# The pace of the second group's output projection beside the first group's FFN, 0.5 to 3.0

## The chip, the cores and the metric

The kernel runs on one core of a Trainium2 chip. The metric is the device time of one execution in microseconds (us); the table below gives the median of three runs and the time of the one execution that was profiled. Engines are named as the profile names them: PE is TensorE (matmuls and transposes), DVE is VectorE, ACT is ScalarE, POOL is GpSimd, SP is the engine that issues most DMAs.

## What is computed

One decoder layer over 1024 prompt tokens and 64 sample tokens, width 1024. Only its end matters here: the mixer's output times `w_out` is added to `x`, then a norm and a SwiGLU FFN (2816 wide) follow, then a last norm.

```python
x = x + mix                                   # mix = mixed @ w_out
hf = rmsnorm(x, norm_ffn)
x = x + (jax.nn.silu(hf @ w_gate) * (hf @ w_up)) @ w_down
...
y_prompt = rmsnorm(xp, norm_final)
y_sample = rmsnorm(xs, norm_final)
```

## The kernel before

The tokens are worked in two groups: group 0 is prompt tokens 0 to 511 (four blocks of 128), group 1 is prompt tokens 512 to 1023 (four blocks, here t4 to t7) and the 64 sample tokens (here s). Every float32 product is made of three matmuls of a high and a low part (`hi*hi`, `hi*lo`, `lo*hi`), so each weight block that is loaded into `wraw` is split: ACT writes `whi` (L223), DVE writes `wlo` (L224). `wraw` has two buffers, `whi` and `wlo` have three each (`WB`, `WH`, `WL`, L64 to L66).

`outproj_b` (L1220) is the second half of the output projection. For each token block it loads `mt` and the earlier sum `x`, transposes `mt` on PE (L1178), and splits the result into `nat_hi` (ACT, L1228) and `nat_lo` (DVE, L1229). Then for each of four column parts c0 to c3 it loads and splits 4 x 256 weights and makes one group of 12 matmuls for each token block (8 for s), which DVE adds to `x` (L1238). Each group needs one of two PSUM banks `pm`.

`ffn_norm` (L1251) then norms each block by `norm_T` (L285): ACT squares and sums (L288), DVE makes the inverse root in nine instructions on one value per row (L213 to L219) and scales the block (`xn`, L289), PE transposes it in eight (L294), ACT writes `act_hi` (L223) and DVE `act_lo` (L224). For s there is a `join` first (L1241).

`ffn` (L1261) makes gate and up products of 24 matmuls each (`pm<-act_hi,whi`, 288 columns wide in group 1: t4, t5 and a quarter of t6 in the first half, the rest and s in the second), then the down product (`pm<-whi,hh`), added to `x` by L1320. In the last block of group 0 the two `w_down` parts stay split in two of the three `whi` buffers until the end, because the token blocks go outermost (t3 to t0, two groups of six matmuls each); after each block `final` norms it: a square on ACT (L1272), the nine DVE instructions, a scaling (L1277) and the store to `y_prompt` from ACT's queue. `far_rows` copies 1.5 MB pieces of `cache_win_v` to the output from SP's queue.

All of this is emitted by Python generators that yield units of estimated work. `beside(main, (side, pace))` (L1385) takes one step of the main generator and lets each side run until it has used pace times the units of that step. The Tile framework then schedules what is emitted, and on each engine the order is fixed in the program. The end of the kernel:

```python
op = pool(st1, "h1", "right")
x2 = op.tile([128, 5, D], F32, name="x2", bufs=1)
out1 = Side(outproj_b(1, op, x2), ffn_norm(1, op, x2), ahead=O7)
beside(dense, (out1, R10))
st0.close()
...
beside(out1, (far, 0.3))
beside(Side(ffn(1, op, x2, hp)), (far, 0.3))
```

`dense` is group 0's chain, of which the last FFN block is left here. What of `out1` is not used up beside `dense` is emitted by the line with `far`. `out1` has 5 x 1.5 + 20 x 1.3 + 5 x 3.0 = 48.5 units.

Of the kernel before, what the change touches and what calls it, by code (L numbers as in the profile page):

```python
# [37 lines left out]
R7 = 1.4  # L38
R8 = 1.1
R9 = 1.07  # L40
R10 = 0.5
R11 = 2.27
R12 = 2.0

# [102 lines left out]
def body(tc, I, O, C, off):  # L147
# [1072 lines left out]
    def outproj_b(F, tp, x2):  # L1220

        hi, lo = act_nat(tp, F)
        for tok in toks(F):
            i, rows, col = tok
            sp.dma_start(x2[:, col // 128], xa[F][col:col + 128])

            def fill(h_, l_, v):
                act.activation(h_, v, AF.Copy, scale=nB)  # L1228
                dve.scalar_tensor_tensor(l_, v, nB, h_.bitcast(F32), op0=OP.mult, op1=OP.subtract)  # L1229
            mixed_T(tp, hi, lo, tok, mix[2 + F][(i % 4) * 128:(i % 4 + 1) * 128] if i < 8 else mixs[1], fill)  # L1230
            yield 1.5
        for c in range(4):
            w = wsplit(w_out[:, 4:8, c * 256:(c + 1) * 256], 4, 256)
            for i, rows, col in toks(F):
                ps = mbank()[:, :256]
                nat_mm(his(hi), his(lo), w, 4, rows, col, ps, True, True)
                xv = x2[:, col // 128, c * 256:(c + 1) * 256]
                dve.tensor_tensor(xv, ps, xv, op=OP.add)  # L1238
                yield 1.3
# [11 lines left out]
    def ffn_norm(F, tp, x2):  # L1251
        wbc = bcast_row(tp, I["norm_ffn"], "wffn")
        hi, lo = act_pair(tp, 576 if F else 512)
        for i, rows, col in toks(F):
            if rows == 64:
                join(tp, x2, True)
            norm_T(tp, x2[:rows, col // 128], rows, wbc, hi, lo, col)
            yield 3.0
        normed[F] = hi, lo
# [125 lines left out]
    def beside(main, *sides, until=None):  # L1385

        left = until
        while main.live and (until is None or left > 0):
            x = next(main.g, None)
            if x is None:  # L1390
                main.live = False
                break
            if until is not None:
                left -= x
            for side, pace in sides:
                side.run(x * pace)
# [89 lines left out]
# [3 lines that stand above are left out]
# [35 lines left out]
```

## Time and profile before

| | us |
|---|---|
| median of three runs (1784.21 to 1785.14) | 1784.65 |
| the profiled execution, its own time | 1786.49 |
| its span in the trace | 1784.7 |
| PE busy in the span | 1697.0 (95%) |
| DVE busy | 1150.2 (64%) |
| ACT busy | 679.4 (38%) |
| mean DMA rate | 182 GB/s |

PE is the busy engine almost everywhere. The time of interest is where group 0's FFN ends and group 1's begins, some 1294 to 1362 us into the span. The granted clock there is given by the profile as a share of the full clock: 1.00 is 2.4 GHz and 0.50 is 1.2 GHz.

### The profile page before, as it was taken

To read this page: it belongs to the slowest core of one execution; us is meant where nothing else is said; L and a number is where in the kernel's file an instruction comes from. 1 tells how busy PE (TensorE), PEld (TensorE's weight loads), DVE (VectorE), ACT (ScalarE), POOL (GpSimd) and SP (SyncE) were. 2 spreads that over 40 slices of the span, in tenths; PEclk is the share of its full clock that TensorE was granted. 3 is DMA by queue.
4 is the path that set the end of the run, shared out by engine and by line. 5 is a ranking of instruction groups with operands and counts; after the bars stand their busy time and mean duration, and the time that the engine had idled before them with its cause. 6 is when DMAs were issued, how large, how long until landed. Compare 5 with 4: busy or idle time off the path is not lost. (4 is left out here: it accounts for less than half of the span.)

```text
span 1784.7 us, 27958 instructions
## 1 busy us (share of the span) xinstructions
PE 1697.0 (95%) x10462; PEld 1464.7 (82%) x10462; DVE 1150.2 (64%) x2829; ACT 679.4 (38%) x1379; POOL 78.2 (4%) x200
## 2 busy tenths in 40 slices
PE   4999999997999999999999989999998999999997
PEld 4988789996766668878887778888887999999996
DVE  6978966866776757797666546676576444343435
ACT  4545434441423353676421134454234223131222
POOL 1000000001001000000011001111100000000000
PEclk9999999998999999999998999999998999999999
DMA  8645556468898867534299678798494333241321
GB/s 272 182 145 159 162 179 171 116 200 271 266 282 256 256 208 225 188 104 118 66 284 287 180 224 256 248 304 274 133 325 154 128 95 95 59 130 36 107 72 65
DMA packets 309569, 324.96 MB, mean 182 GB/s; under 512 B 28221, under 2 KB 260669, under 8 KB 307754
## 3 DMA queue, kind: packets, MB, share of 16 engines
q1 hardware_dynamic: 297754, 275.64, 51.6%
q0 software_dynamic: 10304, 43.08, 6.8%
q10 hardware_dynamic: 1376, 4.46, 0.7%
q8 instruction: 82, 1.34, 0.3%
q14 instruction: 53, 0.43, 0.1%
HBM read 251.31 MB, written 105.63 MB: 200 GB/s over the span
## 5 line engine op out<-in xcount | busy, mean ns | idle before, releaser
L198 PE MATMUL pm<-act_hi,whi 128*128 128x288 f32 (+1 forms) x1056 | 349.4, 331 | 0.2 <-ACT act_hi L223 0.2
L198 PE MATMUL pm<-act_lo,whi 128*128 128x288 f32 (+1 forms) x1056 | 348.1, 330 | 0.0
L198 PE MATMUL pm<-act_hi,wlo 128*128 128x288 f32 (+1 forms) x1056 | 347.4, 329 | 0.0
L223 ACT ACTIVATE whi<-wraw 128x1024 fp32r<-128x1024 f32 x182 | 192.8, 1059 | 381.8 <-PE pm L198 275.8
L224 DVE TENSOR_TENSOR wlo<-wraw,whi 128x1024 fp32r<-128x1024 f32 x182 | 222.3, 1222 | 123.8 <-ACT whi L223 123.3
L198 PE MATMUL pm<-xh,whi 128*128 128x320 f32 (+2 forms) x672 | 230.6, 343 | 11.5 <-ACT whi L223 8.6
L198 PE MATMUL pm<-xl,whi 128*128 128x320 f32 (+2 forms) x672 | 228.4, 340 | 0.1
L198 PE MATMUL pm<-xh,wlo 128*128 128x320 f32 (+2 forms) x672 | 226.7, 338 | 0.2
L198 PEld LDWEIGHTS pm<-act_hi,whi 128*128 128x128 f32 x1056 | 199.2, 189 | 18.4 <-issue 2.1
L198 PEld LDWEIGHTS pm<-act_hi,wlo 128*128 128x128 f32 x1056 | 199.3, 189 | 14.5 <-issue 0.5
L198 PEld LDWEIGHTS pm<-act_lo,whi 128*128 128x128 f32 x1056 | 199.3, 189 | 14.2 <-issue 0.2
L198 PEld LDWEIGHTS pm<-xh,whi 128*128 128x128 f32 x672 | 129.1, 192 | 25.9 <-ACT whi L223 9.1
L1320 DVE TENSOR_TENSOR x<-pm,x 128x256 f32<-128x256 f32 (+1 forms) x148 | 79.9, 543 | 98.2 <-PE pm L198 97.8
L198 PEld LDWEIGHTS pm<-xl,whi 128*128 128x128 f32 x672 | 129.0, 192 | 11.9 <-issue 3.2
L198 PEld LDWEIGHTS pm<-xh,wlo 128*128 128x128 f32 x672 | 128.7, 192 | 10.6 <-DVE wlo L224 1.5
L198 PE MATMUL pm<-own,hh 128*128 128x512 f32 x440 | 129.4, 390 | 0.0
L198 PE MATMUL pm<-whi,hh 128*128 128x256 f32 (+1 forms) x336 | 101.6, 303 | 12.9 <-DVE x L1320 7.6
L198 PE MATMUL pm<-whi,hl 128*128 128x256 f32 (+1 forms) x336 | 99.7, 299 | 0.0
L198 PE MATMUL pm<-wlo,hh 128*128 128x256 f32 (+1 forms) x336 | 99.4, 297 | 0.0
L198 PEld LDWEIGHTS pm<-own,hh 128*128 128x128 f32 x440 | 82.2, 188 | 16.9 <-issue 0.2
L198 PE MATMUL pm<-whi,nat_hi 128*128 128x256 f32 x288 | 83.4, 293 | 1.5 <-DVE n_ss L219 1.1
L1293 ACT ACTIVATE hth<-pm 128x288 f32<-128x288 f32 (+1 forms) x66 | 30.5, 462 | 139.4 <-PE pm L198 139.3
(362 smaller groups left out, 3180.9 us busy)
## 6 DMA issues: line engine op xcount, KB each, us to landing
wraw<-w_in SPq DMA_DIRECT2D x56, 512.0 KB, 4.6
wraw<-w_gate SPq DMA_DIRECT2D x44, 512.0 KB, 3.7
wraw<-w_up SPq DMA_DIRECT2D x44, 512.0 KB, 3.8
wraw<-w_down SPq DMA_DIRECT2D x44, 512.0 KB, 3.6
new_wk_sample<-cache_win_k SPq DMA_DIRECT2D x8, 1536.0 KB, 8.2
qbc<-smp SPq DMA_DIRECT2D x32, 384.0 KB, 7.2
kt<-cache_win_k SPq DMA_DIRECT2D x32, 384.0 KB, 7.0
vt<-cache_win_v SPq DMA_DIRECT2D x32, 384.0 KB, 4.2
```

Source lines behind the costliest of these rows:

```text
L198: pe.matmul(out, lhsT, rhs, start=start, stop=stop)
L223: act.activation(hi, src, AF.Copy)
L224: dve.tensor_sub(lo, src, hi.bitcast(F32))
L1293: act.activation(th, pg[:, :n], AF.Tanh, scale=0.5)
L1320: dve.tensor_tensor(xv, ps, xv, op=OP.add)
```

## The change

One constant, the pace of `out1` beside `dense`:

```diff
-R10 = 0.5
+R10 = 3.0
```

All 48.5 units of `out1` are now emitted within about 16 units of `dense`, and none is left for the line with `far`, so all `far` pieces are emitted beside `ffn(1)`. The program of each engine changes in the following places.

On PE, at the start of group 1's gate and up products (`pm<-act_hi,whi`; `pn<-tab,xn` are the transposes of the norms, t5 and t6 first; t7 is `xn_14144`, s is `xn_14175` before), before:

```order
L294 MATMUL pn_14101<-tab_66,xn_14089 128x128 x4
L294 MATMUL pn_14108<-tab_66,xn_14089 128x128 x4
L294 MATMUL pn_14129<-tab_66,xn_14117 128x128 x4
L294 MATMUL pn_14136<-tab_66,xn_14117 128x128 x4
L198 MATMUL pm_14219<-act_hi_14059,whi_14209 128x288
L198 MATMUL pm_14244<-act_hi_14059,whi_14215 128x288
L294 MATMUL pn_14156<-tab_66,xn_14144 128x128 x4
L198 MATMUL pm_14219<-act_lo_14060,whi_14209 128x288
L198 MATMUL pm_14219<-act_hi_14059,wlo_14210 128x288
L294 MATMUL pn_14163<-tab_66,xn_14144 128x128 x4
```

and now, from t6's transposes on:

```order
L294 MATMUL pn_14090<-tab_66,xn_14078 128x128 x4
L294 MATMUL pn_14097<-tab_66,xn_14078 128x128 x4
L294 MATMUL pn_14117<-tab_66,xn_14105 128x128 x4
L294 MATMUL pn_14124<-tab_66,xn_14105 128x128 x4
L294 MATMUL pn_14156<-tab_66,xn_14144 128x64 x4
L294 MATMUL pn_14163<-tab_66,xn_14144 128x64 x4
L198 MATMUL pm_14216<-act_hi_13991,whi_14206 128x288
L198 MATMUL pm_14216<-act_lo_13992,whi_14206 128x288
L198 MATMUL pm_14216<-act_hi_13991,wlo_14207 128x288
```

Before, the first 48 gate and up matmuls (the first half of the columns) stand ahead of s's transposes; now they stand behind them. In both programs the same number of PE rows, 6330 with four transposes a row, lies ahead of the second half's first matmul.

On PE, at the step from column part c2 to c3 of the output projection, before:

```order
L198 MATMUL pm_13975<-whi_13914,nat_hi_13545 128x256
L198 MATMUL pm_13975<-wlo_13915,nat_hi_13545 128x256
L198 MATMUL pm_13991<-whi_13987,nat_hi_13545 128x256
L198 MATMUL pm_13991<-wlo_13988,nat_hi_13545 128x256
L198 MATMUL pm_13991<-whi_13987,nat_lo_13546 128x256
```

and now (`whi_13735,hh` is a down group of group 0's FFN):

```order
L198 MATMUL pm_13877<-whi_13795,nat_hi_13545 128x256
L198 MATMUL pm_13877<-wlo_13796,nat_hi_13545 128x256
L198 MATMUL pm_13893<-whi_13889,nat_hi_13545 128x256
L198 MATMUL pm_13907<-whi_13735,hh_13352 128x512
L198 MATMUL pm_13907<-wlo_13736,hh_13352 128x512
L198 MATMUL pm_13907<-whi_13735,hl_13354 128x512
L198 MATMUL pm_13907<-whi_13735,hh_13353 128x512
L198 MATMUL pm_13907<-wlo_13736,hh_13353 128x512
L198 MATMUL pm_13893<-wlo_13890,nat_hi_13545 128x256
L198 MATMUL pm_13893<-whi_13889,nat_lo_13546 128x256
```

The eight down groups, which all stood ahead of the output projection's first group, are now spread through it: the last three of them stand behind its last group.

On ACT, at the first squares of group 1's norms (L288), before:

```order
L223 ACTIVATE whi_14209<-wraw_14207 128x1024
L223 ACTIVATE whi_14215<-wraw_14213 128x1024
L288 ACTIVATE xn_14062,n_ss_14061<-x2_13537 128x1024
L288 ACTIVATE xn_14089,n_ss_14088<-x2_13537 128x1024
L223 ACTIVATE act_hi_14059<-pn_14074 128x4x128
L223 ACTIVATE act_hi_14059<-pn_14081 128x4x128
L288 ACTIVATE xn_14117,n_ss_14116<-x2_13537 128x1024
L223 ACTIVATE whi_14335<-wraw_14333 128x1024
```

and now (L1272 is the square of a block of group 0's last norm):

```order
L1272 ACTIVATE xn_13958,n_ss_13957<-x2_7826 128x1024
L288 ACTIVATE xn_13994,n_ss_13993<-x2_13537 128x1024
L288 ACTIVATE xn_14029,n_ss_14028<-x2_13537 128x1024
L1278 DMA y_prompt<-xn_13958 128x1024
L223 ACTIVATE whi_14206<-wraw_14204 128x1024
L223 ACTIVATE act_hi_13991<-pn_14006 128x4x128
L223 ACTIVATE act_hi_13991<-pn_14013 128x4x128
L1272 ACTIVATE xn_14056,n_ss_14055<-x2_7826 128x1024
L288 ACTIVATE xn_14078,n_ss_14077<-x2_13537 128x1024
L223 ACTIVATE whi_14212<-wraw_14210 128x1024
```

Three of the four last norms of group 0, all of which were done before group 1's norms began, now run among them. DVE's program mixes the two kinds in the same way.

## Rows read from the trace of the kernel before

**Rows 1.** The page: busy us of an engine, share of the span.

```profile
PE 1697.0 (95%) x10462; PEld 1464.7 (82%) x10462; DVE 1150.2 (64%) x2829; ACT 679.4 (38%) x1379; POOL 78.2 (4%) x200
```

**Rows 2.** The chain that ended last, in order of time: start, us, what.

```profile
1359.23 1.29 DVE xn L289
1360.65 0.44 PE pn L294 x4
1361.55 411.01 PE pm L198 x2668
```

**Rows 3.** Windows: us, busy PE, PEld, DVE, ACT, POOL, clock, DMA share.

```profile
1336.60:1342.00 5.40, 1.24 (x10) 0.86 (x8) 5.11 (x16) 2.77 (x5) 0.00 (x0) 0.92 1.10 377
1342.00:1349.80 7.80, 3.68 (x16) 3.14 (x16) 7.35 (x24) 3.13 (x6) 0.00 (x0) 0.50 0.31 93
1349.80:1354.80 5.00, 4.38 (x19) 3.99 (x19) 4.49 (x6) 3.98 (x6) 0.95 (x1) 0.50 0.00 0
1354.80:1361.50 6.70, 6.03 (x48) 5.68 (x47) 5.26 (x15) 2.71 (x6) 0.00 (x0) 1.00 0.74 286
```

**Rows 4.** Timeline of PE, 1336 to 1360: start, us, instruction, idle before it.

```profile
1336.47 0.28 PE L198 MATMUL pm<-wlo,nat_hi 128*128 128x256 f32 x1
1338.54 1.09 PE L294 MATMUL pn<-tab,xn 128*128 128x128 f32 x8 [1.79 <-DVE xn L289]
...
1349.83 0.85 PE L198 MATMUL pm<-act_hi,whi 128*128 128x288 f32 x2
...
1354.74 0.34 PE L198 MATMUL pm<-act_hi,wlo 128*128 128x288 f32 x1
...
1358.79 0.30 PE L198 MATMUL pm<-act_hi,whi 128*128 128x288 f32 x1
...
1359.85 0.29 PE L198 MATMUL pm<-act_hi,wlo 128*128 128x288 f32 x1
```

**Rows 5.** Timeline of PE, 1294 to 1312: last gate/up matmul, down, transposes, projection.

```profile
1294.03 0.39 PE L198 MATMUL pm<-act_hi,wlo 128*128 128x512 f32 x1
1294.26 0.39 PE L198 MATMUL pm<-whi,hh 128*128 128x512 f32 x1
...
1294.94 0.60 PE L1178 MATMUL pn<-tab,mt 128*128 128x128 f32 x4
...
1311.47 0.36 PE L198 MATMUL pm<-whi,nat_hi 128*128 128x256 f32 x1 [1.14 <-DVE n_ss L219]
```

**Rows 6.** Timeline of ACT: a weight split, the first `nat_hi`, t4's square.

```profile
1294.28 1.06 ACT L223 ACTIVATE whi<-wraw 128x1024 fp32r<-128x1024 f32 x1 [3.89 <-issue]
...
1295.77 0.67 ACT L1228 ACTIVATE nat_hi<-pn,nB 128x512 fp32r<-128x512 f32 x1
...
1333.87 1.06 ACT L288 ACTIVATE xn<-x 128x1024 f32<-128x1024 f32 x1 [2.69 <-DVE x L1238]
```

**Rows 7.** Timeline of DVE: first `nat_lo`, then t4's and t5's norms.

```profile
1297.12 0.74 DVE L1229 SCALAR_TENSOR_TENSOR nat_lo<-pn,nB,nat_hi 128x512 fp32r<-128x512 f32 x1
...
1335.05 0.15 DVE L214 TENSOR_SCALAR n_ss<-n_ss 128x1 f32<-128x1 f32 x1 [0.88 <-ACT xn L288]
...
1337.20 1.28 DVE L289 SCALAR_TENSOR_TENSOR xn<-x,n_ss,wffn 128x1024 f32<-128x1024 f32 x1
...
1341.30 1.28 DVE L289 SCALAR_TENSOR_TENSOR xn<-x,n_ss,wffn 128x1024 f32<-128x1024 f32 x1
1342.50 0.15 DVE L214 TENSOR_SCALAR n_ss<-n_ss 128x1 f32<-128x1 f32 x1
```

**Rows 8.** Groups by line and form, 1294 to 1362: busy us, mean ns of one.

```profile
L224 DVE TENSOR_TENSOR wlo<-wraw,whi 128x1024 fp32r<-128x1024 f32 x7 | 8.5, 1221 | 0.5 <-ACT whi L223 0.5
L1238 DVE TENSOR_TENSOR x<-pm,x 128x256 f32<-128x256 f32 x20 | 7.7, 416 | 0.0
L1320 DVE TENSOR_TENSOR x<-pm,x 128x512 f32<-128x512 f32 x8 | 5.5, 689 | 0.4 <-PE pm L198 0.3
L1277 DVE SCALAR_TENSOR_TENSOR xn<-x,n_ss,wfin 128x1024 f32<-128x1024 f32 x4 | 5.1, 1278 | 0.0
```

## The prediction

> **What bounds the kernel now.** I read the page first: PE is busy for 95% of the span [rows 1]. Then the chain that ended last: from 1361.55 on it is one piece of 411.01 us of PE matmuls, group 1's FFN [rows 2]. That piece starts at the first matmul of the second half of the columns, behind the transposes of s, which waited for s's scaling `xn` on DVE at 1359.23. In both programs the same PE work lies ahead of this point and behind it. So nearly the whole effect of the change is how far this one point moves; I take the rest of the kernel over unchanged.
>
> Then the stretch before it. The output projection ends on PE at 1336.47 [rows 4]. Until 1349.8 PE then does little but the norms' transposes (1.24 of 5.40 us, then 3.68 of 7.80), while DVE is busy for 5.11 and 7.35 us of the same windows, and the granted clock falls to 0.50 [rows 3]. The stretch is a chain on DVE: five norms, one behind the other. PE gets work back at 1349.83, when the first gate and up matmuls can run on t4, t5 and t6 while t7 and s are still being normed [rows 4]. That looks like a hole of over 13 us for the FFN of group 0 to fill. The question is whether the new order fills it.
>
> **The change, part by part.** Nothing is added or removed; instructions move. I follow the new order in four steps.
>
> *Step 1: when t4's sum is complete.* From 1294.26, the end of group 0's last up product [rows 5], the work on PE up to the end of t4's group in c3 is: 20 transposes in blocks of four at 0.44 [rows 2], 2.2 us; 3 x 56 + 12 = 180 projection matmuls; and 23 down matmuls. A projection matmul takes 0.1185: the order has 212 from the one at 1311.47 to the one at 1336.47 [rows 4, 5], so 25.00 / 211. A down matmul takes 0.23 (1294.03 to 1294.26, [rows 5]). The sum is 2.2 + 21.3 + 5.3 = 28.8, so 1323.1 without waits.
>
> Three kinds of waits are new. (a) At 1294 the down groups stood between the transposes and their use; now each block's transposes are followed by its own projection. The first needs `nat_hi`, done at 1295.77 + 0.67 = 1296.44 [rows 6], against transposes that end at 1294.7: 1.7 us. Its `nat_lo` ends at 1297.86 [rows 7]; by then PE has had 0.24 us of matmuls and 0.44 of transposes since 1296.44: 0.7 us. For the other four blocks ACT and DVE need 0.67 + 0.74 = 1.4 us, against 7 to 10 matmuls (0.8 to 1.2 us) as cover: I take 0.5 each, 2.0. In all 4.4; the bounds are 2.4 (the later blocks covered) and 6.4 (`mt` loads late). (b) and (c) The two `w_down` parts hold two of three `whi` buffers, so the weights of c2 and c3 can be split only when the part before has left PE. A split is 1.06 on ACT [rows 6] and 1.14 on DVE behind it (1221 ns less the 0.08 by which the next instruction starts early: 1341.30 to 1342.50 is 1.20 for a 1.28, [rows 7, 8]). At c2 one down group of 1.38 covers part: 2.2 + 0.2 for handing over - 1.4 = 1.0. At c3 only one matmul stands ahead of the down group, and it needs `whi` itself: 1.06 + 0.2 = 1.25; the down group covers the rest. Together 6.7: t4's sum is complete at about 1329.8.
>
> *Step 2: t4's scaling.* On ACT the square of a final block stands ahead of t4's: two squares of 1.06 [rows 6], with 0.6 for the add, about 1332.5. In before, 2.15 us pass from the first small instruction of t4's norm to its `xn` (1335.05 to 1337.20, [rows 7]). In the new DVE order one final scaling (1.20), three adds L1238 (1.0) and one add L1320 (0.6) stand among them [rows 8], each less 0.08: 4.95. So t4's `xn` starts at about 1337.4, against 1337.20 in before. **The first norm starts no earlier than it did**: what the head start gains is eaten by the waits and by the finals. +0.2.
>
> *Step 3: from t4's scaling to s's.* In before this is 1338.40 to 1359.23, 20.8 us, nearly all DVE busy. The orders of the two programs between these two instructions differ by: three adds L1320 (+1.8), two weight splits more (+1.14 each, of which one replaces the `own` split in before: +1.14), one final scaling (+1.2), 15 more small instructions (at 0.12 where two chains are interleaved: +1.8), two adds L1238 less (-0.7), one gate instruction less (-0.4), and some 1.7 us of DVE waits in before that I take to be filled (of 2.4 us idle in the last three windows of [rows 3]; the rest are gaps inside chains of small instructions). Sum +3.1. Bounds +2 and +5 (the small instructions at 0.2, the waits of 1.7 not filled). s's `xn` then starts at about 1362.5.
>
> *Step 4: the 48 matmuls.* In before the first 48 gate and up matmuls were done while s was normed. Now they stand behind s's transposes on PE, whatever is ready: 48 x 0.1325 (1358.79 to 1359.85 is eight steps, [rows 4]) = 6.4 us that nothing hides. And they start after a stretch in which PE mostly waits. In before the clock was at 0.50 from 1342 until the matmul at 1354.74, 4.9 us after the first gate matmul at 1349.83 [rows 3, 4]. If it is the same now, these 4.9 us do half their work: +2.4, with bounds 0 and 2.5.
>
> The Trainium skill (TensorE: Matmul & The Clock Gate, Part 1) says that the PE clock is gated by how busy PE has been, half rate after idling and full after sustained work. By that the 48 matmuls would begin at half rate, as I have taken it, and the trace of before agrees (0.50 until 1354.74); without it the sum would be 2.4 smaller.
>
> *Sum:* 0.2 + 3.1 + 6.4 + 2.4 = **+12.1 us**. Moved at no cost: the `far` pieces on SP's queue, 1.5 MB each, of which five were issued before group 1's FFN and now none. In that FFN PE ran 411.01 us without a wait [rows 2] beside three of them; with eight, the queue's mean load stays far under the 1.10 of 1336.6 to 1342 [rows 3]. If weights do come late there it adds; I take 0. The stores of the finals move later, behind ACT's squares; they are long done when their buffers are wanted.
>
> The profiled execution took 1786.49 for a span of 1784.7; the median of the runs is 1784.65. I add the sum to the median, as the prediction is for such a median: 1796.7, which I round to **1796.5**. (The profiled one by the same sum: 1798.6.)
>
> **The rivals.**
>
> *Faster: the hole is filled.* From 1336.6 to 1361.55 PE's own work at full clock is 4 x 1.09 + 0.9 for transposes and 6.4 for the 48 matmuls, 11.7 of 24.95 us [rows 2, 4]. If the five norms ran beneath the projection and the down groups, 13.3 would go: 1771. It decides when t4's sum is complete some 15 us earlier than in step 1, or when DVE's list is short: behind t4's sum stand only 44 projection and 25 down matmuls (11.0 us) against over 30 us of DVE work. The order speaks against it. Chance 0.05.
>
> *No change: the early waits don't appear and the clock is up.* Steps 1 and 3 at their lower bounds and no clock term: if the waits of step 1 cost 2.4 + 1 instead of 6.7, t4 starts 3.3 earlier; +0.2 - 3.3 + 2 + 6.4 = +5.3, and if DVE keeps pace throughout, some 2 less: 1788. Chance 0.09.
>
> *Slower still: the clock falls during the projection.* From 1294 to 1307 PE would wait a third of the time. If the granted clock goes to 0.50 there for some 9 us, as it did from 1342 on [rows 3], the roughly 6 us of matmuls in it take 12, partly in place of waits: +5, 1801.5. For it speaks that the clock did fall before 1342, at 0.92 over 1336.6 to 1342; against it, that PE was busy for only 1.24 of the 5.40 us there [rows 3] and would be far busier here. Chance 0.1.
>
> *The change does nothing:* excluded, as the orders differ.
>
> **How the numbers follow.** The forecast has 0.76. The range goes from the no-change case's upper part, 1789.5 (+5), to the clock rival, 1802 (+17), which takes in the bounds of steps 1, 3 and 4. A measurement of this kernel can tell about 0.2%, 3.6 us. Slower by more than that: 0.76 + 0.1 and a part of the no-change case, 0.88. Within: 0.07. Faster: 0.05.
>
> **What would show it.** In the profile after: the long last piece of the chain starts near 1373 instead of 1361.55, with all 48 first gate and up matmuls directly ahead of it and behind s's transposes; PE waits for `nat_hi` and `nat_lo` after 1294 and for `whi` and `wlo` at two places of the projection; t4's `xn` near 1337; the clock 0.50 into the first gate matmuls. The prediction is wrong if t4's `xn` starts much before 1334, or if DVE gets from it to s's in under 20 us, or if group 1's FFN itself shows waits.

## The result and the profile after

The changed kernel takes 1795.57 us (median of 4 runs, 1792.10 to 1798.02), the kernel before, beside it on the same chip, 1784.43 (1778.99 to 1785.14). The ratio is 1.0056 with a 95% interval from 1.0030 to 1.0081: about 11 us slower. The prediction was 1796.5, slower.

Single executions of one kernel differ by several us, more than single terms of the prediction, and nearly all of that arises ahead of the change. So the traces are compared by a stretch that has the change in it: from the start of group 0's last gate or up matmul (1294.03 before, [rows 5]; 1291.68 after) to the start of the second column half of group 1's first gate and up products. Times marked + are us from that first point. Behind the second point both kernels have the same 411.0 us of PE work without a wait, so where the last piece of the chain also holds the 48 matmuls of the first half, 411.0 is taken off its length to find the second point. The first point in the timeline of PE of the changed kernel:

```profile
1291.68 0.39 PE L198 MATMUL pm<-act_hi,wlo 128*128 128x512 f32 x1
```

The chain of waits of the changed kernel, in order of time (start, us, what); it answers to [rows 2]:

```profile
1357.14 1.16 ACT xn L288 x2
1360.25 1.19 DVE xn L289
1361.59 1.09 PE pn L294 x8
1362.68 419.04 PE pm L198 x2716
```

The last piece has 2716 matmuls in place of 2668: the 48 now lie behind s's transposes and nothing hides them. The second half starts at 1362.68 + 419.04 - 411.0 = 1370.7, which is +79.0; before, it was 1361.55, +67.5. The stretch is 11.5 us longer.

The windows of the changed kernel from the norms on (us, busy PE, PEld, DVE, ACT, POOL, clock, DMA share, GB/s); they answer to [rows 3]:

```profile
1337.60:1343.70 6.10, 3.20 (x19) 2.48 (x18) 6.08 (x22) 4.68 (x8) 0.00 (x0) 1.00 0.29 86
1343.70:1351.40 7.70, 1.06 (x8) 0.82 (x8) 7.70 (x20) 2.61 (x5) 0.00 (x0) 0.65 0.60 190
1351.40:1361.50 10.10, 3.91 (x16) 3.14 (x16) 8.98 (x27) 5.63 (x9) 0.95 (x1) 0.50 0.46 167
1361.50:1367.00 5.50, 5.41 (x28) 5.32 (x29) 3.95 (x9) 1.83 (x3) 0.00 (x0) 0.55 0.48 191
...
1372.00:1781.00 409.00, 409.00 (x2659) 385.25 (x2658) 179.88 (x303) 102.39 (x157) 0.00 (x0) 1.00 0.32 100
```

For 18 us, 1343.7 to 1361.5, PE works for 5.0 and DVE for 16.7. Then PE has work again, but starts it at half rate: clock 0.55 until 1367. The last row shows group 1's FFN beside all eight `far` pieces: PE busy for all of 409.00 us.

The waits of PE in the changed kernel, 1290 to 1380 (us in total, times, longest):

```profile
PE pn L294 <- DVE n_ss L218: 9.6, 2, 6.7
PE pn L294 <- DVE n_ss L219: 5.1, 1, 5.1
PE pm L198 <- ACT nat_hi L1228: 1.6, 1, 1.6
PE pn L294 <- DVE act_lo L224: 1.1, 1, 1.1
PE pm L198 <- ACT whi L223: 1.1, 1, 1.1
PE pm L198 <- DVE nat_lo L1229: 1.1, 3, 0.5
PE pm L198 <- DVE wlo L224: 0.8, 1, 0.8
```

Most of it is transposes of norms (L294) that wait for DVE. Why DVE is late is seen in its groups over the stretch (busy us, mean ns, and idle just before them with what ended it); they answer to [rows 8]:

```profile
L1238 DVE TENSOR_TENSOR x<-pm,x 128x256 f32<-128x256 f32 x20 | 8.4, 422 | 9.1 <-PE pm L198 8.9
L1320 DVE TENSOR_TENSOR x<-pm,x 128x512 f32<-128x512 f32 x8 | 5.5, 685 | 1.2 <-PE pm L198 1.1
```

Ahead of the projection's adds (L1238) DVE now stands idle for 9.1 us, waiting for PE; before it was 0.0 in the same group [rows 8]. The projection gives DVE little: one add of 0.42 us for each group of 8 or 12 matmuls. In the kernel before, group 0's down groups had all been issued by +14.5, and DVE worked off their finals under the projection. Now the down groups are spread until +48.7, their finals come late, and DVE idles first and is overloaded after.

### The profile page after: what moved, and what is told of

It reads as the page before. It is cut to its first block, busy times and chain, and to the rows that moved or that the text cites. A ratio compares the mean times of both kernels' runs of the same rounds, so it can differ in the third digit from the quotient of the medians.

```text
span 1793.8 us, 27962 instructions
## 1 busy us (share of the span) xinstructions
PE 1695.6 (95%) x10462; PEld 1463.5 (82%) x10462; DVE 1150.2 (64%) x2829; ACT 678.9 (38%) x1379; POOL 78.5 (4%) x200
## 5 line engine op out<-in xcount | busy, mean ns | idle before, releaser
L1320 DVE TENSOR_TENSOR x<-pm,x 128x256 f32<-128x256 f32 (+1 forms) x148 | 79.7, 543 | 94.7 <-PE pm L198 94.3
L198 PEld LDWEIGHTS pm<-xl,whi 128*128 128x128 f32 x672 | 128.6, 191 | 12.1 <-issue 3.2
L198 PEld LDWEIGHTS pm<-xh,wlo 128*128 128x128 f32 x672 | 128.4, 191 | 10.6 <-DVE wlo L224 1.5
L198 PE MATMUL pm<-wlo,nat_hi 128*128 128x256 f32 x288 | 83.0, 292 | 0.8 <-DVE wlo L224 0.8
```

The source lines that it names most:

```text
L198: pe.matmul(out, lhsT, rhs, start=start, stop=stop)
```

## The experiments

Each edit is shown against the changed kernel unless another one is named. The expectations speak of 79.15 for the stretch of the changed kernel; taken from the chain it is 79.0. Experiments 2, 3, 5 and 8 to 12 ran once each: 1798.84, 1793.12, 1794.48, 1788.77, 1801.90, 1797.87, 1789.87 and 1799.19 us. Such a single time tells little (experiment 2 was expected at 1790.5), as the first point alone differs by up to 12 us between traces, so they are read by the stretch.

**1. s's norm later in the order.**

```diff
-        for i, rows, col in toks(F):
+        for tok in toks(F)[:4]:
...
+        normed[F] = hi, lo, (lambda: norm(*toks(F)[4])) if F else None
...
                     pu = yield from dense_T(*wu, hi, lo, c0, n)
+                    if late:
+                        late()
+                        late = None
```

> The changed kernel, with one thing put elsewhere: the norm of s is emitted inside group 1's FFN, after the first half's gate and up products of the first FF block, so that PE has these 48 matmuls ahead of s's transposes again. The measure is the stretch from the last up matmul of group 0 to the first matmul of the second column half: 67.5 us in the trace of the kernel before, 79.15 in that of the changed kernel, with s's scaling on DVE at +68.5. Theory (the order on PE costs 8.2 us by itself: 48 matmuls that start only when s is normed, part of them at the granted clock of 0.50 to 0.55): s's scaling stays where it is, near +68.5, the 48 matmuls run while DVE norms s, the stretch becomes about 71, and the whole about 1787.5 us (the changed kernel's 1795.6 less 8). Rival (what counts is DVE's delay, and PE's 48 matmuls are late in any order, since they need t4 to t6, whose norms end only at +60): the 48 matmuls start after +62 at half clock and push s's transposes back; the stretch becomes 75 to 79, the whole 1791 to 1795.

Chain of the edited kernel, whose last up matmul of group 0 is at 1288.23:

```profile
1349.22 1.20 DVE xn L289
1351.07 1.97 PE pn L294 x8
1353.04 7.21 PE pm L198 x48
1361.11 410.99 PE pm L198 x2668
```

The 48 matmuls are out of the last piece again and run while DVE norms s. The stretch is 72.9, 6.1 less than in the changed kernel; the time is 1789.86 (10 runs) beside 1785.23, ratio 1.0033 (1.0011 to 1.0054). The 75 of the rival did not come. The 71 of the theory was missed for two reasons. s's scaling came at +69.6 in place of +68.5, the last final scaling having been put ahead of it (+66.9). And the rival's mechanism is there, only smaller: the piece with the 48 matmuls starts at +64.8, takes 7.21 us, and ends 1.2 us after s's scaling was done, so that the chain runs through it and not through s's scaling.

**2. Without group 0's finals.**

```diff
-                    final(*tok)
+                    if F:
+                        final(*tok)
```

> The changed kernel without group 0's final norms (squares, scalings and stores are left out, so y_prompt's first 512 rows are not written). Theory (ACT's squares and DVE's scalings of the finals stand ahead of and among the norms of group 1): t4's scaling starts about 3 us sooner after the last up matmul of group 0 than the +44.6 of the changed kernel, s's scaling some 5 us sooner than +68.5 (four scalings of 1.2 us are gone, and the small instructions with them), and the stretch to the second column half shrinks by the same 5 us, from 79.15 to about 74; the whole about 1790.5. Rival (the down groups on PE, which end late, set the pace, and DVE has slack): the stretch shrinks by under 2 us.

t4's scaling starts at +40.3 (-4.3), s's at +64.9 (-3.6), and the stretch is 75.0, 4 shorter. The finals do stand in the way, for a little less than their DVE time, as the chain shows (last up matmul of group 0: 1298.75):

```profile
1346.29 1.14 DVE wlo L224
1347.49 3.59 DMA wraw<-w_gate
1351.17 1.06 ACT whi L223
1352.26 1.23 DVE wlo L224
1354.13 1.20 DVE xn L289
```

With the scalings gone, DVE came to a weight split of group 1's gate before its weights were there. The load takes 3.59 us and starts when the split before it has freed the `wraw` buffer; t6's scaling stands behind that split on DVE and came 10.9 us after t5's.

**3. PE kept busy between the norms.**

```diff
             norm_T(tp, x2[:rows, col // 128], rows, wbc, hi, lo, col)
+            if F and i in (5, 6, 7):
+                p_ = nbank()
+                for q in range((22, 4, 18)[i - 5]):
+                    mm(p_[:, :256], hi[:, q % 8, 0:128], hi[:, q % 8, 0:256])
```

> The changed kernel with 44 extra matmuls of 128x256 whose result nobody reads: 22 after t5's transposes, 4 after t6's, 18 after t7's, each where PE otherwise waits for the next norm. They add about 10 us of PE time to some 14 us of waiting. Theory (of the 8.2 us that the 48 first gate and up matmuls take after s's transposes, 1.8 come from the granted clock of 0.50 to 0.55 after the stretch of waiting): the clock stays at 1.00 up to these matmuls, they take 6.4 us, and the stretch to the second column half is about 1.8 us shorter, 77.3, if the extra ones do not delay the transposes. Rival (the slow start is something else, such as late weights): 8.2 us again although the granted clock is 1.00.

Windows of the edited kernel: one beside the norms, one with the 48 matmuls.

```profile
1350.00:1361.50 11.50, 8.50 (x44) 7.29 (x44) 9.37 (x29) 5.53 (x9) 0.95 (x1) 0.69 0.39 140
1361.50:1368.30 6.80, 6.80 (x55) 6.73 (x54) 4.05 (x8) 2.02 (x4) 0.00 (x0) 1.00 0.44 157
```

The clock is 1.00 at the 48 matmuls (it was 0.55), and the chain's last piece is 417.35 in place of 419.04: they take 6.35 us where they took 8.0. So 1.7 us of step 4 is the clock, and 6.35 the matmuls themselves. The stretch is only 1.1 shorter (77.9), as s's scaling came 0.9 later; s's transposes, now at full clock too, took 0.68 in place of 1.09.

**4. The projection early, the norms not.**

```diff
-    out1 = Side(outproj_b(1, op, x2), ffn_norm(1, op, x2), ahead=O7)
+    out1 = Side(outproj_b(1, op, x2), ahead=O7)
     beside(dense, (out1, R10))
+    out1.run()
+    out1 = Side(ffn_norm(1, op, x2), ahead=O7)
```

> The half of the change that concerns the output projection: group 1's output projection runs three units for each unit of group 0's FFN, as in the changed kernel, but the norms of group 1 are emitted after the FFN, as most of them are in the kernel before. On PE the first 48 gate and up matmuls then stand mostly ahead of s's transposes. Theory (an early projection gains nothing, because DVE's and ACT's list of finals, norms and splits is the bound; the loss comes from mixing the norms in): the same new waits of about 4.6 us in the projection, all work of PE ends near +44, where it ended in the kernel before (+42.4), t4's scaling at about +46, s's at about +66, the stretch 68 to 70, and the whole within 0.2% of the kernel before, 1785 to 1787.5. Rival (the early projection with its waits is what costs): a stretch of 74 or more, 1791 and up.

The theory fell, and by more than the rival asked for: the stretch is 83.5, the time 1799.51 (4 runs), ratio 1.0085 (1.0060 to 1.0110). The chain (last up matmul of group 0: 1289.89):

```profile
1343.78 1.25 DVE xn L1277
1346.70 1.28 DVE xn L1277
1348.11 1.26 DVE xn L289
...
1371.19 1.20 DVE xn L289
1373.43 410.99 PE pm L198 x2668
```

t4's scaling (L289, 1348.11) comes directly behind the last two finals (L1277), at +58.2. The early projection on its own is harmful; that the norms were emitted among the finals had been a help, since in the changed kernel t4's starts at +44.6.

**5. Experiments 1 and 2 together.**

> Both edits at once: the changed kernel with s's norm emitted after the first half's gate and up products, and without group 0's final norms (their squares, scalings and stores are left out, so y_prompt's first 512 rows are not written). Theory (the loss of 11.6 us has two causes that add up: 48 matmuls behind s's transposes, which the edit of s's norm alone gave back as 6.3 us of stretch, and the finals that stand between the norms, whose removal alone gave back 4.1): the stretch from the last up matmul of group 0 to the second column half, 79.15 in the changed kernel, becomes 68 to 70, about the 67.5 of the kernel before, with s's scaling at +64 to +66. Rival (the two overlap, because without the finals PE's 48 matmuls are late instead, t6's scaling coming at +56.7 behind a late weight split): 71.5 to 73, hardly better than the edit of s's norm alone (72.9).

The stretch is 69.4, with s's scaling at +64.8: the two causes add up (6.1 and 4 by themselves, 9.6 together), and the rival falls. What is left lies within the two traces of the kernel before (67.5 and 69.4, experiment 8). The finals are left out here, not moved, so this shows what they cost in this place and not a way to save it.

**6. A pace of one.**

```diff
-R10 = 3.0
+R10 = 1.0
```

> A smaller dose of the same change: one unit of group 1's output projection and norms for each unit of group 0's FFN (0.5 in the kernel before, 3.0 in the changed one). On PE group 0's last down groups and the projection alternate, the norms' transposes still come after both, and the 48 first gate and up matmuls stand among the norms, ahead of s's transposes. Theory (the loss comes from the order at the end: finals between the norms, and the 48 matmuls behind s): the finals end before the norms begin, the 48 matmuls are covered, and the stretch is 67 to 70, the whole within 0.2% of the kernel before, 1782 to 1788.5. Rival (any head start of the projection pushes the finals into the norms' stretch, as in the kernel whose norms were emitted after the FFN, stretch 83.5): 73 or more, 1791 and up.

The stretch is 66.0, just under the 67 to 70 of the theory, and the rival falls. The time is 1788.35 (10 runs) beside 1788.78, ratio 0.9997 (0.9982 to 1.0013): no difference that can be measured.

**7. The kernel before with columns of 256 and 320.**

```diff
-        cols = [(0, 288), (288, 288)] if F else [(0, 512)]
+        cols = [(0, 256), (256, 320)] if F else [(0, 512)]
```

> The kernel before with group 1's columns cut at 256 and 320 in place of 288 and 288, so that the first half's gate and up products need t4 and t5 alone. Theory (before s is normed, PE is idle for some 13 us, and DVE's list has one wait in it: the FFN's first gate instruction on DVE stands ahead of s's last small instructions and waits 1.16 us for the 48 matmuls): the first of the 48 starts at about +50 in place of +55.8, that wait goes, s's scaling comes at +63.5 to +64 in place of +65.2, and the second half, 0.7 us longer per block but the first as much shorter, starts at +66; the whole about 1 us less, 1784, not to be told from no change. Rival (s's scaling waits for the norms' own chain): the stretch stays 67.5 or grows, as the weight splits and gate instructions of the first products now come ahead of t6's and t7's norms on DVE.

The first of the 48 starts at +50.05, as expected, but the rest went the rival's way: t7's scaling starts at +58.5 (+55.3 before), s's at +66.1, and the second half at +68.7 with a last piece of 414.38 us, which begins at a low clock (0.52 over 1366.5 to 1372.0). The ratio is 1.0018 (1.0005 to 1.0031). Earlier work for PE brought DVE instructions that stand ahead of the norms.

**8 and 9. Both kernels once more.**

> The kernel before once more, unchanged, for the repeatability of the measure: over the seven profiled executions so far the time of group 0's last up matmul lies between 1288.2 and 1299.9 us, although the work ahead of it is the same. Theory (that spread is made in the earlier part and is not the change's): the point moves by several us again, the stretch from it to the second column half is 67.5 within 0.5 us, and the long last piece of the chain 411.0 within 0.1. Rival (the stretch itself varies as much from run to run): off by 2 us or more.

> The changed kernel once more, unchanged, for the same reason. Theory: the stretch is 79.15 within 0.5 us, with t4's scaling at +44.6 and s's at +68.5. Rival (the stretch depends on when the weights for group 1's first products arrive, which differs from run to run): off by 2 us or more, with a wait for w_gate or w_up on ACT that the first profile did not show.

The last up matmul of group 0 came at 1294.47 and 1298.34; over the fourteen traces of this study it lies between 1288.2 and 1299.9. The stretch is 69.4 for the kernel before and 78.7 for the changed one. The changed kernel repeats within 0.4 us, as expected; the one before only within 1.9, more than the 0.5 of the theory and just under the 2 of the rival. Two pieces of its chain account for the 1.9, here in the first trace:

```profile
1316.84 7.10 DMA y_prompt<-xn
1353.75 3.35 PE pm L198 x21
```

and in the second:

```profile
1317.25 7.90 DMA y_prompt<-xn
1354.94 4.47 PE pm L198 x21
```

The store of a final took 0.8 longer to land; the square of a later final waits for it on ACT, and t4's scaling came 0.8 later (+43.9). And the 21 gate and up matmuls took 1.1 longer, as the granted clock rose later (0.80 over +60 to +70, 0.96 in the first trace). The difference of the two stretches is 9.3 in this pair, 11.5 in the first; the medians differ by 11.1.

**10. A pace of two.**

> A dose between: two units of group 1's work for each unit of group 0's FFN. In its order the last of the four final scalings stands just ahead of t4's scaling on DVE, the other three well before, and the 48 first gate and up matmuls stand ahead of s's transposes. Theory (what costs is the finals in the norms' stretch and the 48 matmuls behind s): the 48 are covered and at most one final is in the way; t4's scaling comes at +44 to +46, and the stretch is 68 to 71. Rival (an early projection by itself pushes the finals so late that the norms wait, as in the kernel whose norms were emitted after the FFN, with t4's scaling at +58.2): t4's scaling at +50 or later and a stretch of 75 or more.

The theory fell: the last piece starts at +79.0 although the 48 matmuls lie ahead of s's transposes, and t4's scaling starts at +56.7, the last final just ahead of it at +51.9. The projection itself ended later on PE too, its last matmul at +51.3 (+43.7 in the changed kernel, +42.4 before), behind the last down group. So the list of two causes (the finals, the 48) describes the changed kernel, but is not the rule.

**11. A pace of one and a half, to test a new rule.**

> One and a half units of group 1's work for each unit of group 0's FFN. In its order the 48 first gate and up matmuls stand ahead of s's transposes; group 0's last down groups end some 45 matmul groups earlier than in the changed kernel. New theory, after the kernel with a pace of two lost as much as one with three although its 48 matmuls are covered: what counts is how much of DVE's list is done by the time the projection is over. In the first 40 us after group 0's last up matmul DVE was busy for 31.9 us in the kernel before and 32.9 at a pace of one (stretches 67.5 and 66.0), and for 22.4 at three and 22.7 at two (79.15 and 79.0); what is not done there comes later, one for one, while PE waits. For a pace of one and a half DVE's busy time lies between, 25 to 29 us, and the stretch with it: 31.9 less 22.4 is 9.5 us of DVE for 11.5 of stretch, so 71 to 75. Rival (the old theory: finals between the norms and the 48 matmuls behind s): both are absent here, so 66 to 69.

One row each from the windows of the first 40 us after group 0's last up matmul; behind the length, the third busy time (31.86 in the first row) is DVE's. The kernel before:

```profile
1294.03:1334.03 40.00, 38.69 (x273) 34.73 (x272) 31.86 (x78) 14.66 (x21) 0.00 (x0) 1.00 0.90 322
```
A pace of one:

```profile
1298.24:1338.24 40.00, 38.30 (x272) 34.60 (x271) 32.87 (x78) 15.43 (x22) 0.00 (x0) 1.00 0.87 306
```
One and a half:

```profile
1292.97:1332.97 40.00, 35.77 (x242) 31.42 (x241) 30.35 (x73) 13.65 (x20) 0.00 (x0) 1.00 0.66 225
```
Two:

```profile
1293.99:1333.99 40.00, 34.51 (x218) 30.93 (x217) 22.70 (x49) 9.42 (x14) 0.00 (x0) 0.91 0.51 176
```
Three, the changed kernel:

```profile
1291.68:1331.68 40.00, 35.12 (x252) 31.17 (x251) 22.43 (x48) 11.57 (x17) 0.00 (x0) 1.00 0.47 162
```

Beside the stretches, with the last down group of group 0 on PE and the scalings of its first and last final on DVE:

| kernel | last down group | finals | DVE busy in 40 us | stretch |
|---|---|---|---|---|
| before, pace 0.5 (two traces) | +14.5 | +11.3 to +33.2, to +34.0 | 31.9, 31.1 | 67.5, 69.4 |
| pace 1 | +23.5 | +10.6 to +30.8 | 32.9 | 66.0 |
| pace 1.5 | +33.3 | +15.2 to +40.3 | 30.4 | 70.6 |
| pace 2 | +47.4 | +22.1 to +51.9 | 22.7 | 79.0 |
| pace 3 (two traces) | +48.7, +48.8 | +28.2 to +70.8 | 22.4, 22.4 | 79.0, 78.7 |
| pace 3, norms after the FFN | +49.7 | +29.7 to +56.8 | 21.2 | 83.5 |

The guess of 25 to 29 us for DVE was wrong, 30.35 was measured, and the stretch of 70.6 lies just under the expected 71 to 75, above the rival's 66 to 69. With 30.35 the same line gives 67.5 + (31.9 - 30.35) x 11.5 / 9.5 = 69.4, 1.2 off. In this trace the stretch does not hold the whole loss: the last piece takes 412.42 us in place of 411.0 and begins at a clock of 0.50 (1363.3 to 1366.7). But for 0.3 us the stretch grows in all eight traces of the table as DVE's busy time falls; it is a relation over kernels that differ in more than this one number, not a test of it. The edited kernels outside the table do not follow it: with the same 22.4 us the stretch is 72.9 in experiment 1 and 77.9 in experiment 3, as the order behind the projection counts by itself.

**12. The finals' scalings on GpSimd** (with the edit of experiment 1).

```diff
+                    nc.gpsimd.tensor_scalar(xn[:rows, c], xt[:, c], r, None, op0=OP.mult)
+                    nc.gpsimd.tensor_tensor(xn[:rows, c], xn[:rows, c], wbc[:rows, c], op=OP.mult)
+                    sp.dma_start(dst[:, c], xn[:rows, c])
```

> The changed kernel with s's norm emitted after the first half's gate and up products, and with the scalings of group 0's final norms on GpSimd in place of DVE (two instructions each, and their stores on SP's queue); the squares and the small instructions stay. It computes everything. Theory (DVE's list after the projection sets the time): four scalings of 1.2 us leave it, so the stretch falls from the 72.9 of the same kernel with DVE's scalings by 3.5 to 4.8, to 68 to 69.5, as it did without any finals (69.4), and the changed order then costs at most 2 us against the kernel before (67.5 and 69.4). Rival (it is the chains of small instructions and the splits, not the scalings, or GpSimd's work slows DVE's): 71 or more.

The rival held: the first matmul of the second half comes at +74.4 (72.9 in experiment 1), and from there to the end of the FFN's products PE takes 415.5 us in place of 411.0. Two things are to be seen. First, DVE instructions that run beside GpSimd's can take longer. The timeline of GpSimd (start, us, instruction):

```profile
1339.24 2.67 POOL L1285 TENSOR_TENSOR xn<-xn,wfin 128x1024 f32<-128x1024 f32 x1
...
1367.60 2.37 POOL L1285 TENSOR_TENSOR xn<-xn,wfin 128x1024 f32<-128x1024 f32 x1
```

and of DVE:

```profile
1340.52 1.41 DVE L219 SCALAR_TENSOR_TENSOR n_ss<-n_ss 128x1 f32<-128x1 f32 x1
...
1368.95 2.10 DVE L224 TENSOR_TENSOR own<-wraw,own 128x1024 fp32r<-128x1024 f32 x1
```

A one-element step that takes 0.15 elsewhere took 1.41 and ended with GpSimd's instruction (1341.93 and 1341.91); a split took 2.10 in place of 1.23. The Trainium skill (Trainium Architecture — The Big Picture, What this means for kernel authors) says that DVE and GpSimd share a port pair under an exclusive lock; this trace agrees for GpSimd's product of two tensors (L1285). Beside its other instruction, the scaling by one value per row (L1284, 1364.66 to 1367.51), s's scaling on DVE at 1366.25 took its usual 1.28.

Second, a load of `w_down` came late and took long. SP's queue:

```profile
1369.99 0.36 SPq L1286 DMA_DIRECT2D y_prompt<-xn  x1
...
1371.08 0.52 SPq L228 DMA_DIRECT2D wraw<-w_down  x1
```

and ACT, which splits the weights, waited:

```profile
1378.19 1.06 ACT L223 ACTIVATE own<-wraw 128x1024 fp32r<-128x1024 f32 x1 [8.22 <-DMA wraw<-w_down]
```

The load goes out when DVE's slowed split of the part before is done (1368.95 + 2.10 = 1371.05), as the same load does in experiment 1 (1360.62, behind a split that ends at 1360.60). The store, which waited for GpSimd (1367.60 + 2.37 = 1369.97), was gone 1.1 us earlier and did not hold it. From this load to ACT's split pass 7.1 us, against 4.2 in experiment 1 (1360.62 to 1364.79); why it landed later no run shows. The splits behind it are late, and PE waits for them:

```profile
1380.54 0.40 PE L198 MATMUL pm<-act_hi,whi 128*128 128x288 f32 x1 [0.71 <-ACT whi L223]
...
1382.12 0.40 PE L198 MATMUL pm<-act_hi,wlo 128*128 128x288 f32 x1 [1.04 <-DVE wlo L224]
```

Behind these waits the granted clock is 0.50 for 3.3 us (1383.1 to 1386.4). No run here gives a version that beats both kernels by more than a measurement can tell; the pace of one has the shortest stretch.

## Why the prediction was right, and where it was not

The sign, the place and the size were right: +12.1 was forecast, +11.1 is the difference of the medians, and +11.5 the longer stretch of the trace. That the size is met within 1 us is in part luck: the errors of steps 2 and 3 cancel, and against the second trace of the kernel before the stretch is 9.3 longer, not 11.5. Step by step:

*Step 1, t4's sum.* It was complete at +36.4, against 1329.8 - 1294.03 = +35.8. The waits were smaller than forecast: for `nat_hi` and `nat_lo` 1.6 and 1.1 (4.4 taken, 2.4 the lower bound), for the splits 0.8 and 1.1 (1.0 and 1.25). The wait for `nat_hi`:

```profile
1294.13 0.39 PE L198 MATMUL pm<-whi,nat_hi 128*128 128x256 f32 x1 [1.63 <-ACT nat_hi L1228]
...
1295.56 0.38 PE L198 MATMUL pm<-whi,nat_lo 128*128 128x256 f32 x1 [0.49 <-DVE nat_lo L1229]
```

The four later blocks were nearly covered (0.6 us left of 1.1). That t4's sum was still 0.6 late is PE's own work: from one instruction's start to the next, waits left out, the 181 projection matmuls in the timeline take 23.7 us, 0.131 each, where 0.1185 was taken from a stretch with no waits, transposes or down groups in it. Most steps are 0.12 here too, but some fifteen, next to waits, transposes and down groups, are 0.20 to 0.24.

*Step 2, t4's scaling.* +44.6, against +43.2 before: 1.4 later where 0.2 was forecast. DVE's part was right: 4.9 us from the end of t4's square to the scaling, against 4.95. The square ended 1.2 late, at 1331.33:

```profile
1329.14 1.06 ACT L1272 ACTIVATE xn<-x 128x1024 f32<-128x1024 f32 x1 [3.97 <-DVE x L1320]
...
1331.14 0.19 ACT L288 ACTIVATION_READ_ACCUMULATOR xn<-x 128x1 f32 x1
```

0.6 of it is t4's sum; the rest is mostly that the final's square ahead of t4's waited for its own down add (L1320), which DVE did behind t4's add, where one add of 0.6 had been taken.

*Step 3, t4's scaling to s's.* 22.7 from the end of the one to the start of the other (1337.44 to 1360.18), against 20.8 before: +1.9 where 3.1 was forecast. Steps 2 and 3 together are the forecast +3.3; their errors cancel, which is luck. Experiment 2 shows that the finals are the reason: without them s is 3.6 earlier. The prediction named them in step 2 ("eaten by the waits and by the finals"); it did not see what lies behind them, DVE's idle time under the projection.

*Step 4, the 48 matmuls.* 10.5 us from s's scaling to the second half (+68.5 to +79.0), against 2.3 before: +8.2, forecast 8.8. They cost 8.0, of which experiment 3 shows 6.35 as the matmuls and 1.7 as the clock (6.4 and 2.4 forecast). In the timeline the first 48 run in steps of 0.24 us until 1366.4 and of 0.133 from there, so the low clock lasted some 3.7 us of them, where 4.9 had been taken. The granted clock was 0.50 over 1351.4 to 1361.5, when PE was busy for 3.91 of 10.10 us. The Trainium skill (TensorE: Matmul & The Clock Gate, Part 1) says that PE runs at half rate after idling; this trace agrees.

*No cost for `far`.* Right: 409.00 of 409.00 us of PE.

*The rivals.* "The hole is filled" and "no change" did not come. "The clock falls during the projection" did not come in the changed kernel: 1.00 over the first 40 us. It is not a bad rival, though. Behind the same waits of 1.6 and 0.5 us the clock was 0.70 over +2.5 to +6 in experiment 4 and 0.71 in experiment 10. What it cost there is small: in experiment 4 the projection ended at +45.2 in place of +43.7. Its price of 5 us was too high.

*What stays open.* Why a store lands 0.8 us later and the clock rises later in one trace of the kernel before than in the other; and how much of the pace's effect is DVE's idle time alone, as no run changes it by itself.

## What to carry to other kernels

When an order is changed beside a chain on a second engine, count what the new order leaves that engine to do under the part where PE is the bound: here the early projection gave DVE one add per group, 9.5 us less of its list was done by +40, and the finals came among the norms (4 us of the stretch, experiment 2). Look also at what now stands behind the last wait in PE's program; here independent work put behind a wait cost its full time and began at half rate (8.0 us for 6.35 of matmuls), and putting it ahead gave 6.1 us back with the same list on DVE (experiment 1). A moderate pace, 1 in place of 0.5, changed nothing that can be measured; in single traces most of the loss came between 1.5 and 2, where the last final came behind the projection.

## What the runs showed of the hardware

Whether the granted clock falls behind the same short waits is not settled by the program. In the projection's first us PE has the same instructions and waits in nine of the traces; over +2.5 to +6 it was busy for 3.01 of 3.50 us in the changed kernel, at a clock of 1.00:

```profile
1294.18:1297.68 3.50, 3.01 (x24) 2.77 (x25) 2.50 (x5) 0.69 (x1) 0.00 (x0) 1.00 0.95 332
```

and for as long in experiment 4, at 0.70 (0.71 in experiment 10; 1.00 in the other six):

```profile
1292.39:1295.89 3.50, 3.01 (x16) 2.77 (x17) 2.08 (x4) 0.69 (x1) 0.00 (x0) 0.70 0.87 319
```

The whole work ahead of the change takes from 1288 to 1300 us in fourteen traces, which hides any term of a few us unless it is measured inside one trace. And a DVE instruction on one element a partition can take 1.41 us beside GpSimd, nine times its usual 0.15.
